# Attention and recurrence layer on one core: the values' products of a visit take the first unit in both halves of the array, and the steps' waits are set anew

## The chip, the cores and the metric

The kernel runs on one core of one Trainium2 chip. The metric is the device time of one execution in microseconds (us); the time before is the median of three runs. The profile is of one further execution, whose own time stands beside its span.

## The reference

One decoder layer on 512 positions of width 1024, in float32. One input projection feeds two token mixers and their gates; cut to what matters here:

```python
h = x @ w_in[l] + b_in[l]                       # 5912 columns: q, six k/v parts, gates, f, i, z, gm ...
# mixer A, 8 heads in 2 groups; per block of 128 queries:
ps = masked_softmax(ss, msel[:, :, None])       # "selected" branch: all 8 blocks of 64 are selected at 512 positions
o_slc = jnp.einsum('bghql,bgqld->bghqd', ps, vsel)
pw = masked_softmax(sw, mw)                     # "window" branch, window 512: causal
o_win = jnp.einsum('bghqk,bgkd->bghqd', pw, vw)
o_a = gt[..., 0:1] * o_cmp + gt[..., 1:2] * o_slc + gt[..., 2:3] * o_win
# mixer B: chunkwise gated recurrence (hgrn2) -> o_b, normed and gated
y = sigmoid(gm_a) * (o_a @ w_branch_a) + sigmoid(gm_b) * (o_b @ w_branch_b)
x = layer_norm(alpha * x + y @ w_out[l], ln_g[l], ln_b[l])
```

## The kernel before

**Products.** A weight tile (128 columns of `w_in`, 128x1024 elements as the kernel lays it out) is loaded by SP (`wraw`), copied in a rounded form by ACT (`whi`, L274) and its remainder taken by DVE (`wlo`, L277). A projection is then 24 products on TensorE: for each of 8 parts of the contraction whi by x rounded, whi by x's remainder, wlo by x rounded. 42 tiles of `w_in` and 8 of the branch matrices pass like this; there are two `wraw` buffers, so a tile's load waits until the remainder of the tile two before it is taken. Every operation on TensorE has line 144 (148 for a transpose), since a helper records it; SP's transfers have line 151.

**The weave.** Between the products of the projections stand the steps of all other work: attention, recurrence, norms. Each is a generator; `weave.tick()` is called every six products, and a step that yields n is resumed n ticks later. The table `D` holds these waits by name: `t1.1` is the wait before the values' products of unit 1, `w1.25` that between the ACT copy and the DVE remainder of weight tile 25. So the table sets the order of the instructions on every engine's queue. An engine works off its queue in order.

**Attention.** The four blocks of 128 queries (i = 3, 2, 1, 0) are worked off as six units: for i = 3 and 2 one unit for the selected branch (0) and one for the window branch (1), for i = 1 and 0 one unit with both. Per unit: scores on TensorE, masking with the row minimum on DVE (L738), exponentials on ACT (L755), scaling on DVE (L772) or ACT (L774), transposes on DVE into `big` (L788, L790, L791), and 16 transfers on SP that put the blocks of `big` into a `turn` tile: these turn the probabilities from queries by keys into keys by queries. Only when they have landed can the values' products of that block (a *visit*, function `values`) read them. There are four visits: i = 3 (units 0 and 1), i = 2 (units 2 and 3), i = 1 (unit 4), i = 0 (unit 5).

**A visit.** The values' products are 64x64 pieces: the array's rows 0 to 63 (half 0) and 64 to 127 (half 1) work on different keys, and in each half two column pieces (`ab`) stand side by side, so four products can run at once. Each half has an accumulator of its own (`accs[half]`, a bank of `pso`). A tile is (unit, st); a tile on the diagonal (`j == i`) needs half the queries in one half of the array (`late`, 256 columns in place of 512). Half 0 takes the tiles from the first on, half 1 begins `i + 1` tiles later, which for i = 3 and 2 is the other unit. TensorE takes the products in the order in which they are written.

The lines the steps touch: L816 to L822 (order of a visit's products), L271 to L278 (weight tiles), L800 to L803 (the 16 transfers), L738, L755, L772, L774, L788 to L791 (a unit's probabilities), L828 and L830 (adding a visit's result to `asum`), L999 (a gate tile's tanh, which frees the `pa` bank of its projection).

## Time and profile before

| | |
|---|---|
| median of 3 runs | 411.48 us (410.52 to 412.81) |
| the profiled execution | 412.56 us, of which 410.4 us are its span |
| TensorE (PE) busy | 402.4 us, 98% of the span |
| DVE, ACT busy | 294.0 us (72%), 213.7 us (52%) |
| transfers | 57.60 MB, mean 140 GB/s |
| mean granted TensorE clock | 0.994 |

PE is one product after the other nearly throughout, so the question in each stretch is whether something keeps it from going on; the busy shares of the others matter only there. A matmul's record runs on until its result is written and overlaps the next, so the step from one start to the next says what a product costs, not the duration of its record. One float32 product of a visit is two records.

### The profile page before, as it was taken

To read this page: it belongs to the slowest core of one execution; us is meant where nothing else is said; L and a number is where in the kernel's file an instruction comes from. 1 tells how busy PE (TensorE), PEld (TensorE's weight loads), DVE (VectorE), ACT (ScalarE), POOL (GpSimd) and SP (SyncE) were. 2 spreads that over 40 slices of the span, in tenths; PEclk is the share of its full clock that TensorE was granted. 3 is DMA by queue.
4 is the path that set the end of the run, shared out by engine and by line. 5 is a ranking of instruction groups with operands and counts; after the bars stand their busy time and mean duration, and the time that the engine had idled before them with its cause. 6 is when DMAs were issued, how large, how long until landed. Compare 5 with 4: busy or idle time off the path is not lost.

```text
span 410.4 us, 6085 instructions
## 1 busy us (share of the span) xinstructions
PE 402.4 (98%) x2119; PEld 325.0 (79%) x2119; DVE 294.0 (72%) x675; ACT 213.7 (52%) x442; POOL 5.2 (1%) x17
## 2 busy tenths in 40 slices
PE   9999999999999999999998999999999999999994
PEld 8888888899888887778873878885867888888884
DVE  5906599787665888899999586866432879882773
ACT  3445461643225645786785596981223758458211
POOL 2000000001100000000000000000000000000000
PEclk9999999999999999999998999999999999999999
DMA  7975820143332423471184364364938861053121
GB/s 257 381 237 205 290 79 0 36 150 90 113 94 84 136 79 128 114 196 55 60 212 151 102 176 133 105 204 110 243 99 268 256 198 59 0 168 140 41 112 51
DMA packets 27182, 57.60 MB, mean 140 GB/s; under 512 B 5905, under 2 KB 8337, under 8 KB 27153
## 3 DMA queue, kind: packets, MB, share of 16 engines
q1 hardware_dynamic: 26720, 56.84, 44.5%
q10 hardware_dynamic: 432, 0.39, 0.3%
q8 instruction: 16, 0.26, 0.3%
q14 instruction: 14, 0.11, 0.1%
HBM read 42.12 MB, written 2.10 MB: 108 GB/s over the span
## 4 chain that ended last, share of the span: by engine, by line
PE 84%; DVE 7%; SPq 4%; DMA 2%; issue 1%; ACT 1%; DVEq 0%; ACTq 0%
PE pa L144 53%; PE pss L144 14%; PE pso L144 13%; PE pst L144 4%; SPq L151 4%; DVE t L738 2%; DVE wlo L277 1%; DMA turn<-big 1%; DVE big L788 1%; DVE t L512 1%; DVE t L513 1%; DMA t<-t 0%; ACT t L755 0%; PE pst L148 0%; DVE t L695 0%
## 5 line engine op out<-in xcount | busy, mean ns | idle before, releaser
L144 PE MATMUL pa<-t,whi 128*128 128x512 f32 x640 | 199.8, 393 | 0.0
L144 PEld LDWEIGHTS pa<-t,whi 128*128 128x128 f32 x640 | 118.3, 188 | 29.1 <-issue 4.4
L144 PE MATMUL pa<-t,wlo 128*128 128x512 f32 x320 | 124.7, 390 | 0.0
L277 DVE TENSOR_TENSOR wlo<-wraw,whi 128x1024 fp32r<-128x1024 f32 x44 | 53.6, 1217 | 52.2 <-ACT whi L274 48.8
L274 ACT CAST whi<-wraw 128x1024 fp32r<-128x1024 f32 x44 | 45.9, 1045 | 59.7 <-PE pa L144 50.4
L144 PEld LDWEIGHTS pa<-t,wlo 128*128 128x128 f32 x320 | 60.1, 188 | 12.8
L755 ACT ACTIVATE t<-t,sm_mn 128x512 f32<-128x512 f32 (+3 forms) x64 | 35.2, 553 | 13.3 <-DVE sm_mn L738 13.2
L144 PE MATMUL pso<-t,t 128*128 128x512 f32 (+2 forms) x158 | 33.2, 349 | 0.1
L144 PE MATMUL pss<-t,t 128*128 128x512 f32 (+2 forms) x158 | 30.2, 324 | 0.0
L144 PEld LDWEIGHTS pso<-t,t 128*128 128x128 f32 x158 | 25.8, 198 | 3.9 <-ACT t L233 0.4
L144 PE MATMUL pa<-t,t 128*128 128x512 f32 (+1 forms) x104 | 27.2, 367 | 0.0
L144 PEld LDWEIGHTS pss<-t,t 128*128 128x128 f32 x158 | 23.8, 190 | 2.8
L788 DVE STREAM_TRANSPOSE big<-t 128x512 f32<-128x512 f32 (+3 forms) x48 | 23.4, 523 | 0.4 <-PE pss L144 0.4
L144 PEld LDWEIGHTS pa<-t,t 128*128 128x128 f32 x104 | 18.4, 188 | 3.1
L774 ACT ACTIVATE t<-t,sm_mn 128x128 f32<-128x128 f32 (+3 forms) x39 | 18.0, 522 | 5.0 <-DVE sm_mn L766 4.9
L144 PE MATMUL pso<-turn,t 64*64 64x512 f32 (+1 forms) x160 | 19.1, 599 | 1.4 <-DMA turn<-big 1.4
L144 PE MATMUL pa<-turn,t 128*128 128x512 f32 x64 | 19.9, 389 | 0.0
L144 PE MATMUL pss<-t,whi 128*128 128x512 f32 x64 | 19.7, 389 | 0.0
L201 ACT CAST t<-t 128x512 fp32r<-128x512 f32 x16 | 9.6, 619 | 19.0 <-DVE t L1017 9.8
L144 PEld LDWEIGHTS pso<-turn,t 64*64 64x64 f32 x160 | 6.9, 142 | 13.2 <-issue 11.0
L144 PE MATMUL pst<-t,t 128*128 128x512 f32 (+2 forms) x80 | 15.1, 345 | 0.0
L999 ACT ACTIVATE t<-pa,hbias 128x512 f32<-128x512 f32 x16 | 10.9, 680 | 8.1 <-PE pa L144 8.1
(201 smaller groups left out, 520.9 us busy)
## 6 DMA issues: line engine op xcount, KB each, us to landing
wraw<-in_wf_dram SPq DMA_DIRECT2D x38, 512.0 KB, 3.5
turn<-big SPq DMA_DIRECT2D x48, 128.0 KB, 3.2
wraw<-in_wbr_dram SPq DMA_DIRECT2D x8, 512.0 KB, 4.2
t<-in_wout_dram SPq DMA_DIRECT2D x16, 256.0 KB, 4.5
turn<-big SPq DMA_DIRECT2D x32, 96.0 KB, 2.2
t<-in_wi_dram SPq DMA_DIRECT2D x8, 256.0 KB, 4.8
big<-in_w_dram SPq DMA_DIRECT2D x8, 256.0 KB, 6.4
t<-t SPq DMA_DIRECT2D x32, 64.0 KB, 2.0
```

The lines of the kernel that those rows point to most:

```text
L144: return tc.keep_in_program_order(nc.tensor.matmul(*a, **k))
L151: tc.keep_in_program_order(nc.sync.dma_start(o, i))
L201: A.copy(dst_hi, src)
L274: A.copy(hi, raws[i])
L277: V.tensor_tensor(lo, raws[i], hi.bitcast(F32), ALU.subtract)
L512: V.transpose(sqT, osq[h][1])
L513: V.tensor_reduce(part[:, 16 * h:16 * h + 16], sqT.rearrange("p (c d) -> p c d", d=32), AX.X, ALU.add)
L738: V.tensor_tensor_reduce(out=p[:, c], in0=pg[ab][:, 256 * z:][:, c], in1=amask[:, 512 - n:512], op0=ALU.add, op1=ALU.min, scale=-0.125, sc ...
L755: A.activation(p, p, AF.Exp, bias=mn[:, h:h + 1], scale=-1.0, accum_out=den[:, h:h + 1])
L774: A.mul(p, p, d)
L788: V.transpose(to, of)
L999: A.activation(gm[name], ps, AF.Tanh, bias=hbias[:, m:m + 1], scale=0.5)
```

## The change

In `values` each half gets a list of its own: the tiles in the order first unit, second unit, for both halves (for i = 0 half 1 takes them backwards), with `at`, the columns that half has worked off so far. The products of both halves are then written in the order of `at`. The tiles, products and sums are the same. The table `D` is new in about half of its entries. It has the same steps, and the same instructions come out of it, in another order, but for three scalings of 128x128 which stand on ACT in place of DVE. Lines of the changed file are one higher than before up to L810, five higher behind `values`.

```diff
-D = dict(h0=6, h2=6, h3=14, h4=0, h5=7, h6=9, n0=20, n1=4, n2=4, n3=1, n4=3, c0=3, c1=5, c2=2, c3=0, r0=5, p0=2,
+D = dict(h0=6, h2=6, h3=14, h4=0, h5=7, h6=9, n0=20, n1=4, n2=4, n3=0, n4=3, c0=4, c1=5, c2=4, c3=0, r0=5, p0=2,
...
         accs = PO(), PO()
-        for n in range(len(tiles)):
-            for half in range(2):
-                v, st = tiles[(n + half * (i + 1)) % len(tiles)]
+        todo = []
+        for half in range(2):
+            at = 0
+            for n, (v, st) in enumerate(tiles if i else tiles[::1 - 2 * half]):
                 br, j = units[v][1][st // (i + 1)], st % (i + 1)
                 late = 2 * (j == i and half != br)
-                for ab in range(2):
-                    rows, c = slice(64 * half, 64 * half + 64), (128, NV)[br] * br + 64 * ab
-                    T.matmul(accs[half][64 * ab:64 * ab + 64, 128 * late:512], vts[j][rows, c:c + 64],
-                             probs[v][rows, st, late:4, 128 * ab:128 * ab + 128],
-                             start=n == 0, stop=n == len(tiles) - 1)
+                todo.append((at, n, half, v, st, br, j, late))
+                at += 4 - late
+        for at, n, half, v, st, br, j, late in sorted(todo):
+            for ab in range(2):
+                rows, c = slice(64 * half, 64 * half + 64), (128, NV)[br] * br + 64 * ab
+                T.matmul(accs[half][64 * ab:64 * ab + 64, 128 * late:512], vts[j][rows, c:c + 64],
+                         probs[v][rows, st, late:4, 128 * ab:128 * ab + 128],
+                         start=n == 0, stop=n == len(tiles) - 1)
```

**TensorE in the visit of i = 3, before.** `pso_2294` is the bank of half 0, `pso_2295` that of half 1; `turn_1874` holds unit 0, `turn_2107` unit 1.

```order
L144 MATMUL pso_2294<-turn_1874,t2_1019 64x512 x2
L144 MATMUL pso_2295<-turn_2107,t2_1019 64x512 x2
L144 MATMUL pso_2294<-turn_1874,t2_1038 64x512 x2
L144 MATMUL pso_2295<-turn_2107,t2_1038 64x512 x2
L144 MATMUL pso_2294<-turn_1874,t2_1071 64x512 x2
L144 MATMUL pso_2295<-turn_2107,t2_1071 64x512 x2
L144 MATMUL pso_2294<-turn_1874,t2_1137 64x512 x2
L144 MATMUL pso_2295<-turn_2107,t2_1137 64x512 x2
```

The same place now; `turn_1807` holds unit 0, `turn_2091` unit 1.

```order
L145 MATMUL pso_2294<-turn_1807,t2_1019 64x512 x2
L145 MATMUL pso_2295<-turn_1807,t2_1019 64x512 x2
L145 MATMUL pso_2294<-turn_1807,t2_1040 64x512 x2
L145 MATMUL pso_2295<-turn_1807,t2_1040 64x512 x2
L145 MATMUL pso_2294<-turn_1807,t2_1071 64x512 x2
L145 MATMUL pso_2295<-turn_1807,t2_1071 64x512 x2
L145 MATMUL pso_2294<-turn_1807,t2_1139 64x512 x2
L145 MATMUL pso_2295<-turn_1807,t2_1139 64x256 x2
L145 MATMUL pso_2295<-turn_2091,t2_1019 64x512 x2
L145 MATMUL pso_2294<-turn_2091,t2_1019 64x512 x2
```

Unit 1 was read by the third product of the visit (its second row) and is now first read by the seventeenth. The visit stands at the same place among the projections' products as before.

**SP around unit 1's transfers, before.** `wraw_2104` is weight tile 25 (the gate tile gb1), `wraw_2171` and `wraw_2250` tiles 26 and 27; `t2_1870` is a step of the recurrence's norm.

```order
L151 DMA wraw_2015<-in_wf_dram 128x1024
L151 DMA t2_1870<-t2_1870 32x64 x8
L151 DMA wraw_2104<-in_wf_dram 128x1024
L151 DMA turn_2107<-big_1109 32x1024 x16
L151 DMA wraw_2171<-in_wf_dram 128x1024
L151 DMA wraw_2250<-in_wf_dram 128x1024
```

The same place now; tile 25 is `wraw_2125`, tile 26 `wraw_2170`, tile 27 `wraw_2250`.

```order
L152 DMA wraw_2019<-in_wf_dram 128x1024
L152 DMA t2_1893<-t2_1893 32x64 x8
L152 DMA turn_2091<-big_1127 32x1024 x16
L152 DMA wraw_2125<-in_wf_dram 128x1024
L152 DMA wraw_2170<-in_wf_dram 128x1024
L152 DMA wraw_2250<-in_wf_dram 128x1024
```

The load of tile 25 has moved from ahead of the 16 transfers to behind them.

**DVE at the remainder of tile 25, before** (`wlo_2221`). It stands between the maskings of a visit of scores (L738), and the eight transposes of unit 2 (L788) come 26 instructions later, with the remainder of tile 26 behind them.

```order
L738 ISA t2_2225,sm_mn_2195<-pss_2194,t2_321 128x384
L738 ISA sm_mn_2195 128x1
L277 TENSOR_TENSOR wlo_2221<-wraw_2104,whi_2176 128x1024
L738 ISA t2_2227,sm_mn_2204<-pst_2202,t2_321 128x384
L738 ISA sm_mn_2204 128x1
```

The same step now (`wlo_2184`):

```order
L789 STREAM_TRANSPOSE big_1127<-t2_2065 128x3x4x32
L789 STREAM_TRANSPOSE big_1127<-t2_2067 128x3x4x32
L789 STREAM_TRANSPOSE big_1127<-t2_2069 128x3x4x32
L278 TENSOR_TENSOR wlo_2184<-wraw_2125,whi_2176 128x1024
L278 TENSOR_TENSOR wlo_2393<-wraw_2170,whi_2379 128x1024
L833 TENSOR_TENSOR asum_340<-asum_340,pso_2295 128x4x4x32
```

The remainder of tile 25 now stands behind the last of the eight transposes of unit 2. On TensorE tile 25 is the next projection but the rest of one (12 products) behind the visit, as before.

## The prediction, made before the change was run

> **What bounds the kernel now.** The page's first part and its chain of work come first:

> ```profile
> span 410.4 us, 6085 instructions
> PE 402.4 (98%) x2119; PEld 325.0 (79%) x2119; DVE 294.0 (72%) x675; ACT 213.7 (52%) x442; POOL 5.2 (1%) x17
> PE 84%; DVE 7%; SPq 4%; DMA 2%; issue 1%; ACT 1%; DVEq 0%; ACTq 0%
> ```

> PE works 402.4 of 410.4 us. No other engine can bound the whole; a change can win only where PE waits or is slow, and lose only where it makes PE wait. Between 150 and 330 us, where all visits lie, the view of waits has one line for PE:

> ```profile
> PE pso L144 <- DMA turn<-big: 1.4, 1, 1.4
> ```

> It is the visit of i = 3. PE's timeline (start, busy time, what, idle time before it) and the table of stretches (busy time of each engine, then the granted clock) show it:

> ```profile
> 214.78 0.39 PE L144 MATMUL pa<-t,wlo 128*128 128x512 f32 x1
> 215.10 1.08 PE L144 MATMUL pso<-turn,t 64*64 64x512 f32 x4
> 217.55 8.35 PE L144 MATMUL pso<-turn,t 64*64 64x512 f32 x60 [1.37 <-DMA turn<-big]
> 225.84 0.72 PE L144 MATMUL pa<-t,whi 128*128 128x512 f32 x2
> ...
> 228.71 0.62 PE L144 MATMUL pa<-t,whi 128*128 128x512 f32 x2
> 229.16 0.39 PE L144 MATMUL pa<-t,wlo 128*128 128x512 f32 x1
> ```

> ```profile
> core 0: us, PE busy (x) PEld busy (x) DVE busy (x) ACT busy (x) POOL busy (x), PEclk, DMA share, GB/s
> 211.14:214.55 3.41, 3.41 (x16) 2.81 (x15) 3.41 (x12) 2.85 (x8) 0.00 (x0) 1.00 0.99 222
> 214.55:217.96 3.41, 2.04 (x11) 0.62 (x13) 3.40 (x12) 2.96 (x9) 0.00 (x0) 1.00 0.88 198
> 217.96:221.38 3.42, 3.42 (x20) 1.29 (x16) 3.42 (x8) 3.42 (x7) 0.00 (x0) 0.50 0.80 309
> 221.38:224.79 3.41, 3.41 (x38) 1.46 (x32) 3.41 (x8) 0.49 (x1) 0.00 (x0) 1.00 0.02 5
> 278.25:283.13 4.88, 4.88 (x49) 1.74 (x48) 2.96 (x9) 0.00 (x0) 0.00 (x0) 1.00 0.19 62
> 299.68:302.84 3.16, 3.16 (x33) 1.12 (x32) 0.00 (x0) 0.00 (x0) 0.00 (x0) 1.00 0.41 101
> ...
> 402.28:405.70 3.42, 2.40 (x21) 2.20 (x19) 0.91 (x4) 1.12 (x5) 0.00 (x0) 1.00 0.00 0
> ```

> The visit starts at 215.10. Four records run, all in half 0, because the next instruction in PE's queue is half 1's first and it reads unit 1, which has not landed. PE goes on at 217.55 and is back at the projections at 225.84: 10.74 us. In the stretch 217.96 to 221.38 the granted clock is 0.50, with PE busy all through. The stretch before it is the one with the wait, PE busy 2.04 of 3.41.

> **Term 1: what the visit loses.** The visits of i = 2 and i = 1 are undisturbed (the fifth and sixth row of the table, clock 1.00): 4.88 and 3.16 us. Their tile steps per half, counting a 256-column tile as half a step, are 5.5 and 3.5, so a step is (4.88 − 3.16)/2 = 0.86 us. Visit 3 has 7.5 steps, two more than i = 2: 4.88 + 2 × 0.86 = 6.60 us. It takes 10.74, so 4.14 us are lost: 1.37 waiting, 3.42/2 = 1.71 at half clock, and the rest, 1.06, on a start in which one half stood still.

> With the new order unit 1 is first read by the seventeenth product, half 1's at about 215.10 + 4 steps × 0.86 = 218.5. Has it landed by then? Before, half 1's first product of unit 1 was let go at 217.55 (it needs only part of the sixteen transfers), and the last transfer was issued so (the SP queue: start, time, what):

> ```profile
> 205.57 0.50 SPq L151 DMA_DIRECT2D wraw<-in_wf_dram  x1
> 206.12 10.41 SPq L151 DMA_DIRECT2D turn<-big  x16
> 216.63 11.02 SPq L151 DMA_DIRECT2D wraw<-in_wf_dram  x3
> DMA to landing us min/median/max: 2.7/3.5/4.6
> DMA to landing us min/median/max: 3.0/3.5/6.9
> ```

> The first landing line is that of the transfers of this window, the second that of all weight loads. The last issue ends at 216.53; now the load of tile 25 is behind and not ahead, which makes every issue 0.55 us earlier and takes 512 KB from in front of them. I expect the last to land at 218.4 to 218.9, about when it is read: wait 0 to 0.4. Term 1 is −4.14, if nothing else waits. A wait of 0.4 there would only eat from the next one, below.

> **Term 2: the remainder of tile 25.** DVE's queue (and ACT's copy of the next tile) around it:

> ```profile
> 208.96 1.43 DVE L533 COPY t<-t 128x512 f32<-128x512 f32 x4 [0.61 <-ACT t L526]
> 211.90 1.23 DVE L277 TENSOR_TENSOR wlo<-wraw,whi 128x1024 fp32r<-128x1024 f32 x1
> 213.04 0.55 DVE L738 CUSTOM_DVE_ANT_0 t<-pst,t 128x384 f32<-128x384 f32 x1
> 222.39 3.79 DVE L788 STREAM_TRANSPOSE big<-t 128x384 f32<-128x384 f32 x8
> 226.10 1.19 DVE L277 TENSOR_TENSOR wlo<-wraw,whi 128x1024 fp32r<-128x1024 f32 x1
> 227.21 0.68 DVE L828 TENSOR_TENSOR asum<-asum,pso 128x512 f32<-128x512 f32 x1
> 220.84 1.03 ACT L274 CAST whi<-wraw 128x1024 fp32r<-128x1024 f32 x1
> 228.68 1.05 ACT L274 CAST whi<-wraw 128x1024 fp32r<-128x1024 f32 x1 [2.55 <-PE pa L144]
> 229.63 0.68 ACT L999 ACTIVATE t<-pa,hbias 128x512 f32<-128x512 f32 x1
> ```

> From 208.96 on DVE is never idle (3.41, 3.40, 3.42, 3.41 us of the four stretches above). The remainder of tile 25 was taken at 211.90 and costs 213.04 − 211.90 = 1.14 in the queue. Now it stands behind the eight transposes of unit 2. These end at 226.10 − 1.14 = 224.96, and the remainder 1.19 later, at 226.15. Its inputs are no limit: load of tile 25 issued at about 216, landed by 219.5 (median 3.5), ACT's copy at about 220.8, where that of tile 26 was.

> PE needs it for the third product of tile 25's projection. Before, that stood at 229.16, 3.32 us after the visit's end. The visit now ends at 215.10 + 6.60 = 221.70, so PE asks at 225.02 and waits until 226.15: **1.1 to 1.2 us**. This is a new wait where before DVE was 16 us ahead. The bounds: 0, if DVE's queue shortens by more than it seems (the two scalings and copies around it are not all the same length), to 1.7, if the transposes start half a microsecond later, behind ACT's last scaling. I take 1.15, since the DVE rows fill the time without a gap. Queued behind the waiting PE are only projections; behind the late remainder on DVE stand that of tile 26, needed six microseconds later, and the sum of the visit's result. From 226.15 on PE is 4.14 − 1.15 = 2.99 us ahead of before.

> **Term 3: tile 27.** Its load waits for the remainder of tile 25 and so moves from 217.5 (the second of the three in SP's last row) to about 226.2; at the median it lands at 229.7, the copy (1.05) and the tanh behind it in ACT's queue (0.68; it frees a `pa` bank) are done at about 231.4. PE needs that bank for the projection that began at 236.35 before:

> ```profile
> 236.35 0.73 PE L144 MATMUL pa<-t,whi 128*128 128x512 f32 x2
> ```

> so now at 233.4: 2 us to spare. Zero, with a bound of 1.3 (a landing of 6.9 us).

> **Term 4: the other visits.** i = 2 and i = 1 show no wait and clock 1.00 before; the order of their products changes nothing there, and unit 3's and 4's transfers had landed before their visits by microseconds. That of i = 2 is taken 12 products (2.7 us) earlier, i = 0 24 later; three scalings go from DVE to ACT, which is busy 52%. Zero, between −0.2 and +0.4 (small groups between projections cost about 0.1 each: 0.72 against 0.62 for the first pair behind one).

> **Sum.** The profiled execution took 412.56 us (span 410.4 and 2.2 around it). 412.56 − 4.14 + 1.15 + 0 + 0 = **409.6**. It lies 1.08 above the median of the runs shown; some of that may lie outside the visit and would not be in a median of the changed kernel. I take a quarter off, 0.3, as a guess: **409.3**, 0.5% under 411.48.

> [...] After the visit's wait the clock fell, and the wait was 1.37 us in a stretch with 2.04 of 3.41 busy; at 402.28 a stretch with 2.40 of 3.42 busy was followed by none. The new wait leaves 2.25. [...]

> **Rivals.**
> - **B, no wait for tile 25** (DVE's queue turns out over a microsecond shorter, or ACT hides it). For: sizes on DVE vary by several hundredths each, and the four stretches hold 37 of them. Against: four stretches without a gap. 412.56 − 4.14 − 0.3 = 408.1; with a rest of the wait 408.5.
> - **C, the clock halves after the new wait.** For: the row above, 2.04 against 2.25. Against: 2.40 did not. One stretch of 3.42 at 0.50: +1.7, 411.0.
> - **D, the change doesn't do what it says**: unit 1 lands later than 218.5 by more than 1.2 us. For: landing up to 4.6 behind the issue, and both halves then wait with all the array. A wait of 1.2 is absorbed in that for tile 25; from there on it adds, and the clock falls as before: about 409.3 + 1.7 = 411.0, up to 411.5.
> - **E, slower: the load of tile 27 comes late.** It is issued 8.7 us later than before, and ACT's queue holds the tanh that frees a bank behind its copy. From a landing of 5.5 us after the issue on PE waits at 233.4, with half a clock stretch after it as in the visit; above about 7.8 us (2.3 + 1.7 = 4.0) the time is 413.3 to 414. For: one weight load took 6.9. Against: the median is 3.5, and little else is in flight (DMA share 0.02 from 221.38 to 224.79; before, only tile 28's load followed).

> **The numbers.** Forecast A (a wait of 0.8 to 1.5 for tile 25, clock whole) 0.46, B 0.22, C 0.14, D 0.10, E 0.08. A's own range is 408.8 to 410.2. About 0.5% (2.06 us) is what a measurement of this kernel can tell from no change: faster is below 409.42, slower above 413.54. A lies on the border, 0.25 faster and 0.21 same; B is faster (0.21); C and D are nearly all same (0.23); E 0.08 slower. Faster 0.46, same 0.46, slower 0.08. The range reaches from B to C and D: 407.9 to 411.5, leaving out E and the ends of B, C and D, some 0.17.

> **What would show it.** Right: no wait of `pso` for `turn<-big` at 215 to 219; the visit in 6.5 to 6.8 us at clock 1.00; a new wait of PE for `wlo` (DVE, L278) of about 1.1 us at 225; tile 27's load at about 226; nothing else new among PE's waits. Wrong: a stretch at 0.50 after 225 (C), a wait for `turn` at the seventeenth product (D), no wait for `wlo` (B), a wait of PE for ACT's L1004 near 233 (E). The forecast as a whole falls if PE's busy time before 205 us or after 240 changes by over half a microsecond.

## The result, and the profile after the change

| | before | changed |
|---|---|---|
| median of 10 executions | 411.61 us (410.44 to 412.98) | 409.39 us (408.75 to 409.66) |
| ratio | | 0.9944, interval 0.9927 to 0.9960 |
| the profiled execution | 412.56 us, span 410.4 | 408.75 us, span 406.9 |

The change is faster by 2.2 us, 0.56%. 409.3 had been forecast. In 26 of the 68 later timed executions of the kernel before, the mean granted clock was 0.991 to 0.995 and the time 412.3 to 415.1 (median 413.0); the other 42 have a median of 410.8 (two of them are over 413 at a clock of 0.998). The profiled execution, 412.56, is one of those with a half-clock stretch. Ten of ten executions of the change have 0.995 to 0.998 and lie within 0.9 us.

The page's head and the chain of work of the changed kernel:

```profile
span 406.9 us, 6079 instructions
PE 399.4 (98%) x2119; PEld 323.5 (80%) x2119; DVE 294.0 (72%) x672; ACT 215.1 (53%) x445; POOL 4.9 (1%) x17
PE 90%; DVE 7%; issue 1%; DMA 1%; ACT 0%; DVEq 0%; ACTq 0%
```

SP's queue, 4% of the chain before, is gone from it. PE's waits between 150 and 330 us are one again, but another one:

```profile
PE pa L145 <- DVE wlo L278: 1.0, 1, 1.0
```

PE's timeline at the visit and behind it (start, busy time, what, idle time before), then the table of stretches with the granted clock:

```profile
214.36 6.67 PE L145 MATMUL pso<-turn,t 64*64 64x512 f32 x64
220.96 0.74 PE L145 MATMUL pa<-t,whi 128*128 128x512 f32 x2
...
223.85 0.61 PE L145 MATMUL pa<-t,whi 128*128 128x512 f32 x2
225.45 0.50 PE L145 MATMUL pa<-t,wlo 128*128 128x512 f32 x1 [0.98 <-DVE wlo L278]
...
232.77 0.73 PE L145 MATMUL pa<-t,whi 128*128 128x512 f32 x2
```

```profile
214.55:217.96 3.41, 3.41 (x38) 1.34 (x36) 3.41 (x10) 3.33 (x9) 0.00 (x0) 1.00 0.89 252
217.96:221.38 3.42, 3.42 (x36) 1.33 (x29) 3.42 (x7) 3.26 (x6) 0.00 (x0) 1.00 0.40 153
221.38:224.79 3.41, 3.09 (x14) 2.18 (x12) 3.41 (x8) 0.32 (x1) 0.00 (x0) 1.00 0.00 0
224.79:228.20 3.41, 2.75 (x12) 2.30 (x13) 2.94 (x4) 0.00 (x0) 0.00 (x0) 1.00 0.51 165
```

All 64 records of the visit run without a gap: 220.96 − 214.36 = 6.60 us, where it took 10.74, and the clock is whole. Then PE waits 0.98 us for tile 25's remainder. From the third product's normal step (0.45, as between 228.71 and 229.16 before) to the 1.60 between 223.85 and 225.45 it loses 1.15; the first steps behind the wait cost another 0.1.

DVE's and SP's queues at the same place:

```profile
213.41 0.56 DVE L739 CUSTOM_DVE_ANT_0 t<-pso,t 128x384 f32<-128x384 f32 x1
220.49 3.79 DVE L789 STREAM_TRANSPOSE big<-t 128x384 f32<-128x384 f32 x8
224.20 2.33 DVE L278 TENSOR_TENSOR wlo<-wraw,whi 128x1024 fp32r<-128x1024 f32 x2
```

```profile
203.91 10.91 SPq L152 DMA_DIRECT2D turn<-big  x16
DMA to landing us min/median/max: 2.3/2.4/3.0
```

The remainders of tiles 25 and 26 stand behind the transposes, as the order says. The first of unit 1's 16 transfers is issued 2.2 us earlier than before, and the issue of the last ends 1.7 us earlier (214.82 against 216.53); 0.7 of both is the earlier start of the visit itself. They land in 2.4 us at the median in place of 3.5.

The difference of the two profiled executions is 3.8 us. 0.8 of it is no work of the change: it stands in the first products of the kernel, which both have alike (12 products, first row before, second after):

```profile
4.19 2.63 PE L144 MATMUL pso<-t,t 128*128 128x256 f32 x12
4.09 1.91 PE L145 MATMUL pso<-t,t 128*128 128x256 f32 x12
```

The changed kernel itself shows both: in a second profile of it (`after2`) the same products take 2.72 us. The trace's record of the full clock begins at 6.34 us in the kernel before, at 4.58 in the change and at 6.89 in `after2` (what was granted ahead of that isn't recorded, and the tables of stretches show 1.00 there). In all 14 traces the 12 products take 1.88 to 1.95 us where it begins by 4.64, 2.41 and 2.47 where it begins at 5.75 and 5.88, and 2.63 to 2.85 where it begins at 6.34 or later. So this part of the difference goes with the moment at which the full clock came.

From just ahead of the visit (214.78 before, 214.04 after) to the projection behind the next scores (236.35 and 232.77) the change wins 3.58 − 0.74 = 2.84 us: 4.14 in the visit, less 1.3 at the new wait and its neighbourhood.

### The profile page after: what moved, and what is told of

Its sections match the earlier page's. It is cut to its first block, busy times and chain, and to the rows that moved or that the text cites. A ratio compares the mean times of both kernels' runs of the same rounds, so it can differ in the third digit from the quotient of the medians.

```text
span 406.9 us, 6079 instructions
## 1 busy us (share of the span) xinstructions
PE 399.4 (98%) x2119; PEld 323.5 (80%) x2119; DVE 294.0 (72%) x672; ACT 215.1 (53%) x445; POOL 4.9 (1%) x17
## 4 chain that ended last, share of the span: by engine, by line
PE 90%; DVE 7%; issue 1%; DMA 1%; ACT 0%; DVEq 0%; ACTq 0%
PE pa L145 60%; PE pss L145 15%; PE pso L145 11%; PE pst L145 4%; DVE big L789 2%; DVE t L739 1%; DVE wlo L278 1%; DMA turn<-big 1%; DVE t L541 1%; DVE t L535 0%; DVE t L534 0%; PE pst L149 0%; DVE t L542 0%; DVE big L1130 0%; DVE t L696 0%
## 5 line engine op out<-in xcount | busy, mean ns | idle before, releaser
L278 DVE TENSOR_TENSOR wlo<-wraw,whi 128x1024 fp32r<-128x1024 f32 x44 | 53.4, 1216 | 35.1 <-ACT whi L275 35.1
L1004 ACT ACTIVATE t<-pa,hbias 128x512 f32<-128x512 f32 x16 | 10.9, 681 | 12.0 <-PE pa L145 11.9
L145 PE MATMUL pso<-turn,t 64*64 64x512 f32 (+1 forms) x160 | 16.4, 552 | 0.0
L739 DVE CUSTOM_DVE_ANT_0 t<-pss,t 128x128 f32<-128x128 f32 (+3 forms) x24 | 10.2, 474 | 7.7 <-PE pss L145 7.7
```

The lines of the kernel that those rows point to most:

```text
L145: return tc.keep_in_program_order(nc.tensor.matmul(*a, **k))
L278: V.tensor_tensor(lo, raws[i], hi.bitcast(F32), ALU.subtract)
L739: V.tensor_tensor_reduce(out=p[:, c], in0=pg[ab][:, 256 * z:][:, c], in1=amask[:, 512 - n:512], op0=ALU.add, op1=ALU.min, scale=-0.125, sc ...
L1004: A.activation(gm[name], ps, AF.Tanh, bias=hbias[:, m:m + 1], scale=0.5)
```

## The experiments

### The order alone, and the table alone

`order_only` has the new `values` with the old `D`, `table_only` the new `D` with the old `values`. No other line differs.

> The new order of the visits' products with the old table. Theory 1 (the loss sat in the order): unit 1 is first read by the seventeenth product, about 3.4 us into the visit, and was let go 2.5 us into it before, so the visit takes 6.6 to 7.0 us at clock 1.00 instead of 10.74; the remainder of tile 25 stands where it stood, so PE does not wait for it: 407.6 to 408.4 us, ratio to before 0.990 to 0.993, faster than the whole change. Theory 2 (the new table is needed, since unit 1's last transfers land too late for the seventeenth product): a wait of 0.3 to 1 us there, perhaps with half clock behind it: 409.5 to 410.5.

Measured: 408.72 us, ratio 0.9926 (0.9901 to 0.9951), 0.3 above the range of theory 1. PE's visit, and the weight load that starts half 1 (PEld):

```profile
215.13 7.48 PE L144 MATMUL pso<-turn,t 64*64 64x512 f32 x64
215.13 0.19 PEld L144 LDWEIGHTS pso<-turn,t 64*64 64x64 f32 x4 [0.35 <-issue]
215.96 0.23 PEld L144 LDWEIGHTS pso<-turn,t 64*64 64x64 f32 x8 [0.63 <-DVE sm_mn L738]
```

And DVE ahead of that point:

```profile
211.93 1.23 DVE L277 TENSOR_TENSOR wlo<-wraw,whi 128x1024 fp32r<-128x1024 f32 x1
...
215.34 0.56 DVE L738 CUSTOM_DVE_ANT_0 t<-pso,t 128x384 f32<-128x384 f32 x1
```

Theory 1 names the direction and not the size. There is no wait for tile 25 and no half clock, but the visit takes 7.4 to 7.5 us. Half 1 starts 0.83 us after half 0, although nothing of unit 1 is read yet: its accumulator, a `pso` bank, is still being masked by DVE until 215.90. One half works in the meantime, so PE shows no idle time, and only PEld's row tells it.

> The new table with the old order of the products. Theory 1 (the order is what counts): half 1's first product still reads unit 1 at once and waits, the visit takes 9 to 10.7 us with half clock behind it: 411 to 412, ratio 0.998 to 1.000. Theory 2 (the earlier transfers would have done by themselves): unit 1 is let go about 1 us into the visit (in the profile of the change its first reader's releaser came 1.0 us after the visit's start), the four records that run alone cover that, the visit takes 7.0 to 7.5 us at clock 1.00, and the time that it loses is taken from the wait for tile 25's remainder, which shrinks from 1.0 to 0.1 to 0.6: 409.2 to 409.9, ratio 0.994 to 0.996, the same as the change.

Measured: 409.53 us, ratio 0.9962 (0.9941 to 0.9983).

```profile
214.50 1.07 PE L145 MATMUL pso<-turn,t 64*64 64x512 f32 x4
216.37 6.66 PE L145 MATMUL pso<-turn,t 64*64 64x512 f32 x60 [0.79 <-DVE t L535]
```

Theory 2 comes nearer in the time and is wrong in its working. Half 1 waited until 216.37, so the visit took 8.5 us and not 7.0 to 7.5. The releaser that the row names, a transpose of the recurrence, writes nothing that this product reads; its inputs are unit 1's transfers, one of which, issued at 213.42, landed at 215.99 in the trace, and PE's weight-load queue went on from its wait for that one at 216.02. So it is to be read as those. One of the 12 executions, 412.22 at a clock of 0.994, had the half clock all the same, so the old order had not lost that risk. No wait for `wlo` remained at all: the 1.9 us that the visit lost had covered it. So with the new table the old order costs almost nothing in the end (409.53 against 409.4), since the wait behind the visit takes what the visit gives. And with the old table the new order alone was no slower than the whole change (408.72 against 409.39 and 409.48, with executions that overlap). Both parts pay for one and the same thing.

### Where the remainder of tile 25 stands

`rem_first` lets unit 2's transposes start behind the remainder:

```diff
+                        if x == 0 and v == 2:
+                            while 25 not in rem:
+                                yield 1
+                            with tc.issue_after(rem[25].ins):
+                                V.transpose(to, of)
```

> The changed kernel with the remainder of tile 25 on DVE ahead of the eight transposes of unit 2 instead of behind them. Theory 1 (the remainder's place is the whole cause of the new wait): PE's wait for wlo is gone, 1.0 to 1.3 us less than the change: 408.1 to 408.4, ratio to before 0.991 to 0.992. Theory 2 (the transposes, now 1.2 us later, hold up unit 2's transfers and the wait comes back later): a new wait of PE of about 1 us further on, 409.4.

Measured: 407.71 us, ratio 0.9909 (0.9878 to 0.9940). It was run again beside the change on one chip:

> The changed kernel with the remainder of tile 25 ahead of unit 2's transposes, again, to compare with the change on the same chip: 407.7, that is 1.2 to 1.7 us under the change.

> The changed kernel itself, beside the next one on the same chip: 409.4, visit 6.60 to 6.67 us, a wait of about 1.0 for tile 25's remainder.

Measured: 408.09 (407.78 to 408.37) against 409.48 (408.76 to 409.95), 1.4 us less, and every execution of the one is under every one of the other. The view of waits has no line for PE between 150 and 330 us in either profile of it. The first one's DVE and PE:

```profile
214.36 6.67 PE L145 MATMUL pso<-turn,t 64*64 64x512 f32 x64
220.50 1.22 DVE L278 TENSOR_TENSOR wlo<-wraw,whi 128x1024 fp32r<-128x1024 f32 x1
221.63 1.04 DVE L792 STREAM_TRANSPOSE big<-t 128x384 f32<-128x384 f32 x2
222.58 1.19 DVE L278 TENSOR_TENSOR wlo<-wraw,whi 128x1024 fp32r<-128x1024 f32 x1
...
225.21 1.94 DVE L792 STREAM_TRANSPOSE big<-t 128x384 f32<-128x384 f32 x4
```

Theory 1 holds: the place of the remainder is the whole of the new wait. The transposes end at 227.15 in place of 224.28, and nothing waits for them. This version beats both kernels.

### What the new table gives the visit

The change's visit takes 6.60, that of the order alone 7.48. `order_rem` keeps the old table and new order and moves only the remainder out of the maskings, to just ahead of unit 2's transposes (`last[4]` is the last masking of that visit of scores; the transposes wait as in `rem_first`):

```diff
+        while i == 25 and 4 not in last:
+            yield 1
+        if i == 25:
+            with tc.issue_after(last[4].ins):
+                rem[i] = V.tensor_tensor(lo, raws[i], hi.bitcast(F32), ALU.subtract)
```

> The new order with the old table, as before, and the remainder of tile 25 on DVE moved from among the maskings to just ahead of unit 2's transposes. With the old table alone the visit took 7.48 us, 0.8 more than in the change, and the start of half 1 was held until the maskings on DVE had released its bank. Theory 1 (the remainder, 1.14 us, was what made these maskings late): half 1 starts with half 0, and what is left is unit 1's last transfer, which landed at about 219.1 and is now asked for at 218.6 to 219.0: visit 6.7 to 7.2 us, 407.9 to 408.4. Theory 2 (something else holds half 1): the visit stays at 7.5 and the time at 408.7.

Measured: 408.88 us, no better than the order alone. PE's row and PEld's in the visit:

```profile
215.16 7.39 PE L144 MATMUL pso<-turn,t 64*64 64x512 f32 x64
215.16 0.21 PEld L144 LDWEIGHTS pso<-turn,t 64*64 64x64 f32 x8 [0.35 <-DVE sm_mn L744]
...
218.17 0.22 PEld L144 LDWEIGHTS pso<-turn,t 64*64 64x64 f32 x4 [0.23 <-issue]
219.30 0.24 PEld L144 LDWEIGHTS pso<-turn,t 64*64 64x64 f32 x8 [0.90 <-issue]
```

The mechanism was right, the gain missed. Both halves start at 215.16 now, eight weight loads at once. But then a step takes 1.13 us (218.17 to 219.30) where the others take 0.43: the 0.8 us are lost there instead, where unit 1 is first read. `order_rem_load` moves the load of tile 25 behind unit 1's transfers as well (`load_behind` yields until they are issued):

```diff
+        if i + 3 == 25:
+            weave.start(load_behind(i + 3))
+        else:
+            load(i + 3)
```

> As the run before this one with the old table (new order, remainder of tile 25 just ahead of unit 2's transposes), and the load of tile 25 behind unit 1's 16 transfers on SP. There half 1 started at once, but the visit took 7.39 us, as unit 1 was let go at 218.07 (half 1) and 219.19 (half 0), where a visit without waits asks at 218.2 and 218.6. Theory 1 (the load ahead of them, 0.55 us of issue and 512 KB, is what made the transfers late): they come 0.6 us or more earlier, visit 6.6 to 6.8 us, 408.1 to 408.3. Theory 2 (they are late for what comes before them): the visit stays at 7.3 to 7.4 and the time at 408.9.

Measured: 408.02 us, ratio 0.9897 (0.9863 to 0.9931). First the visit, then SP's transfers and their landing in `order_rem`, then in this run:

```profile
214.78 6.67 PE L144 MATMUL pso<-turn,t 64*64 64x512 f32 x64
```

```profile
206.58 10.44 SPq L151 DMA_DIRECT2D turn<-big  x16
DMA to landing us min/median/max: 2.8/3.8/4.8
```

```profile
204.91 10.26 SPq L151 DMA_DIRECT2D turn<-big  x16
DMA to landing us min/median/max: 2.2/2.4/3.3
```

Theory 1 holds: with the load out of their way the transfers land in 2.4 us at the median and not 3.8, and the visit has no gap. Their issues also come earlier: against the start of the visit the first by 1.3 us and the end of the last by 1.5, more than the 0.55 of the load's own issue. Which of the two made up the 0.7 us isn't shown, since the one move brought both. So two steps of the whole new table carry the visit beside its order: the remainder out of the maskings and the load behind the transfers. With the old table these two, the remainder being ahead of the transposes, give the time of `rem_first` (408.0 against 407.7 and 408.1).

### The other visits

`i3_only` is the change with the new order for i = 3 alone.

> The changed kernel, but only the visit of i = 3 has the new order; i = 2, 1 and 0 have the old one. Theory 1 (their order is worth nothing, as term 4 has it): the time of the change, 409.4 within 0.4. Theory 2 (part of the gain is theirs): 0.5 us or more above it, 409.9 and up, with a wait of PE in one of these visits.

Measured: 409.44 us (409.04 to 409.65). The order of the other three visits is worth nothing that shows. Its profile has the visit of i = 3 at 6.79 us and the wait for `wlo` at 1.36.

### When the clock falls

`rem_x2` takes the remainder of tile 25 twice; `wait1` and `wait2` repeat one transpose of unit 2 once and twice. Each only lengthens PE's wait for it.

> The changed kernel with the remainder of tile 25 taken twice by DVE, so that PE waits 1.0 + 1.14 = 2.1 us for it with the whole array. Theory 1 (the clock falls only behind a stretch of 3.41 us that is idle throughout): the time is 409.4 + 1.14 = 410.5 in all runs, granted clock 1.00 behind the wait. Theory 2 (it falls behind a stretch that is busy for only 60%, as the profile before shows): 2.1 us idle leave a stretch at 38 to 60% in about 8 of 10 positions of the stretch, so most runs have a stretch at half clock, +1.7: about 412.2.

> The changed kernel with one of unit 2's eight transposes done twice, so that PE waits 0.98 + 0.46 = about 1.45 us for tile 25's remainder, with the whole array. Theory 1 (the clock falls behind a stretch of 3.41 us of which about half is unused; 1.6 us idle would fit 7 of 10 runs at a wait of 2.2): no run with half clock, all granted clocks 0.995 or more, 409.9 us. Theory 2 (1.37 us idle are enough, as the profile of the kernel before reads at first sight): a wait of 1.45 lies wholly in one stretch in 57% of its positions, so some 6 of 10 runs have a clock of 0.993 to 0.994 and 411.6 us.

> The same with that transpose done three times, a wait of about 1.9 us. Theory 1 (1.6 us idle in a stretch are needed): half clock in about 60% of the runs, these at 412.0, the others at 410.3. Theory 2 (1.37 are enough): in about 75%. Theory 3 (a stretch that is idle throughout is needed, and the falls at a wait of 2.2 had another cause): in none.

| kernel | wait of PE | executions with clock 0.993 to 0.995 and over 411.5 us | their median | median of the others |
|---|---|---|---|---|
| the change | 0.98 | 0 of 10 | | 409.4 |
| `wait1` | 1.45 | 0 of 10 | | 409.7 |
| `wait2` | 1.92 | 5 of 10 | 411.8 | 410.2 |
| `rem_x2` | 2.24 | 7 of 10 | 412.0 | 410.3 |

The profiled execution of `wait2` has such a stretch (columns as in the prediction's table):

```profile
225.27:228.68 3.41, 1.50 (x7) 1.09 (x7) 3.41 (x6) 0.00 (x0) 0.00 (x0) 1.00 0.13 18
228.68:232.10 3.42, 3.42 (x10) 2.64 (x9) 1.30 (x3) 1.40 (x2) 0.00 (x0) 0.50 0.83 281
```

Behind this wait of 1.92 us the granted clock is 0.50 for 3.42 us, and PE was busy for 44% of the stretch before (1.50 of 3.41 us). That stretch was not idle throughout, so theory 1 of `rem_x2` and theory 3 of `wait2` fell. What came is theory 1 of `wait1` and `wait2`; theory 2, that 1.37 is enough by itself, fell in `wait1` (6 of 10 expected, none seen).

The traces also suggest why only a part of the executions was hit. In all 14, the first record of the full clock lasts a whole number of stretches of 3.413 us (62 of them in the kernel before, 6.34 to 217.96, and 117 in the change, 4.58 to 403.94), so the edges of the stretches are known for each profiled execution; they lie elsewhere against the program each time. In the profiled execution of `rem_x2` (full clock from 3.81 us on) an edge divides the wait of 2.24 into 1.23 and 1.01, and the clock stays whole:

```profile
222.26:225.67 3.41, 2.18 (x10) 1.46 (x8) 3.38 (x7) 0.00 (x0) 0.00 (x0) 1.00 0.00 0
225.67:229.08 3.41, 2.40 (x10) 1.99 (x11) 3.29 (x4) 0.00 (x0) 0.00 (x0) 1.00 0.36 123
229.08:232.50 3.42, 3.42 (x19) 2.64 (x19) 1.37 (x2) 2.46 (x4) 0.00 (x0) 1.00 0.57 184
```

Taken stretch by stretch, one with 0.98 us of idle time (the change), one with 1.02 (the kernel before, 402.28 to 405.70) and the two of `rem_x2` were followed by the full clock; one with 1.91 (`wait2`), one with 2.84 (the change, 400.53 to 403.94) and one without any work of PE (the kernel before, 405.70 to 409.11) were followed by half. Between these lie two that do not agree. The stretch of the visit before has 1.37 us idle and was followed by 0.50. The wait of `i3_only` (full clock from 5.88 us on) is as long, also lies within one stretch, and did no harm:

```profile
224.33:227.75 3.42, 2.06 (x10) 1.38 (x9) 3.42 (x6) 0.00 (x0) 0.00 (x0) 1.00 0.12 25
227.75:231.16 3.41, 3.41 (x17) 2.82 (x16) 1.21 (x3) 1.33 (x2) 0.00 (x0) 1.00 0.89 270
```

Why, then, did the visit before fall? Its stretch also holds 1.08 us in which only half 0 worked. To see whether a part-used array counts as idle, `quarters` writes the visit's products quarter by quarter:

```diff
+        seq = [(x, ab) for x in sorted(todo) for ab in range(2)]
+        if i == 3:
+            seq.sort(key=lambda z: (z[0][2], z[1]))
```

> The changed kernel, with the products of the visit of i = 3 written so that the four quarters of the array are used one after the other: first all of half 0's first column piece, then its second, then half 1's. PE is never idle, but only a quarter of the array works, for 4 x 6.6 = about 26 us. Theory 1 (the clock goes by how much of the array is used, so that the half-used start of the visit before counted with its 1.37 us of idle time): stretches at 0.50 within the visit, which then lasts up to 50 us. Theory 2 (only idle time counts): granted clock 1.00 throughout, about 429 us in all.

Measured once: 423.8 us. The visit and two of its stretches:

```profile
214.53 21.84 PE L145 MATMUL pso<-turn,t 64*64 64x512 f32 x64
220.80:224.20 3.40, 3.40 (x12) 1.04 (x8) 3.40 (x8) 0.42 (x1) 0.00 (x0) 1.00 0.00 0
231.00:234.50 3.50, 3.50 (x12) 1.20 (x9) 0.00 (x0) 0.00 (x0) 0.00 (x0) 1.00 0.02 7
```

The clock is 1.00 all through the visit: theory 1 falls, and a quarter of the array at work without idle time did not lower the clock here. (The visit took 21.84 us and not 26, so a product whose quarter works alone took about a sixth less than one of four: 4 × 6.60 would be 26.4.) But theory 2, that idle time alone counts, does not fit the kernel before beside `i3_only` and `wait1`: 1.37 us idle halved its clock, and 1.36 in one stretch and 1.45 in ten executions did not. In its other executions the wait may have been longer, since it hangs on the landing of unit 1; no trace of them shows it, and the profiled one fell with 1.37 itself. Why is open.

## Why the prediction was right, point by point

**The time** was 409.39; the sum gave 409.6 and the forecast 409.3. That it came within 0.1 is in part luck: two profiles of the change differ by 1.2 us already at the start of the visit (214.36 and 215.59). Against the profiled execution it forecast −3.0 (before the 0.3), and 2.84 stand between the traces from the visit to behind the next scores. The gain of the medians is smaller, 2.2, because three in five executions before (42 of 68) have no half-clock stretch. Against these (410.8) the change wins 1.4: the visit's wait and half-filled start, 1.37 + 1.06, less the new wait's 1.3, makes 1.1, if they lost as much there as the profiled one; no profile of such an execution shows it. The term of 1.71 for half clock belonged only to the profiled execution and those like it, and the prediction counted it whole. The guess of 0.3 for what lies outside the visit went the right way between these two profiles, whose starts differ by 0.8; it was a guess, and `after2` starts later than the profile before. The prediction also named a sign by which it would fall as a whole, that PE's busy time before 205 us or after 240 changes by over half a microsecond. That did not come: PE is busy 204.14 and 204.23 us up to 205, though it is 0.7 us further on with its work at the visit, which is the start again. From the projection behind the next scores to PE's last product both profiles take 168.3 us.

**Term 1** was right to the hundredth: 6.60 us, 4.14 less. The reason given for it was not. It took the order of the products to be enough, "if nothing else waits". Two things else would have waited. The bank of half 1 was masked until 215.9 before, behind the remainder of tile 25, which stood in DVE's queue among these maskings; so part of the 1.06 put down to unit 1 was the bank's, and the order alone leaves 0.8 (`order_only`). And unit 1's transfers were judged by "0.55 us earlier": with the load ahead of them they cost 0.7 (`order_rem`), and with it behind they are issued 1.3 to 1.5 us earlier against the visit and land 1.4 us sooner after their issue (`order_rem_load`). The prediction treated the remainder's move only as a cost. It was also what made the visit whole.

**Term 2** was right: 0.98 us of waiting, 1.15 in the step, where 1.15 was forecast, at 225.45 where 226.15 was forecast (0.7 of which is the earlier start of the execution). That DVE's queue is its whole cause is shown by `rem_first`. Rival B fell.

**Term 3** and rival E: the load of tile 27 was issued at 225.4, and ACT's copy waited for it, as said; the tanh behind it ended at 230.45, 2.3 us before PE's 232.77 (2 forecast):

```profile
228.82 1.05 ACT L275 CAST whi<-wraw 128x1024 fp32r<-128x1024 f32 x1 [7.12 <-DMA wraw<-in_wf_dram]
229.77 0.68 ACT L1004 ACTIVATE t<-pa,hbias 128x512 f32<-128x512 f32 x1
```

The load had landed within 3.4 us of its issue, where E needed 5.5. What a late one would have cost was not tried.

**Term 4** was right: `i3_only` has the time of the change.

**Rival C and the row.** Rival C did not come, in ten executions. The row read alone, 1.37 us idle, was too strict for a wait with the whole array at work: 1.36 within one stretch (`i3_only`) and 1.45 in ten executions (`wait1`) cost nothing. A longer one did cost clock: the profile of `wait2` has 3.42 us at 0.50 behind a stretch that was busy for 1.50 of 3.41 us.

**Rival D** fell: unit 1 was never waited for in the change.

## What to carry to other kernels

When a stall is removed, look at what it had been covering, and at every resource of the first instruction behind it (its input, its accumulator's bank, its weights), since the profile names only the last to come; here the bank stood behind the input, and each would have cost the visit 0.7 to 0.8 us with the new order. A step that is moved out of one queue's way can be put back in a third place: the remainder belonged neither among the maskings nor behind the transposes but between them. And before a gain is counted against one profiled execution, see whether other executions have the same stall at the same price.
